# Softmax reciprocals: a 128x512 broadcast turned by four transposes, against 8 columns turned once and spread through DRAM

## The chip, the core and the metric

The kernel runs on one core of a Trainium2 chip. A core has five engines, each with a queue of its own that it works through in order: TensorE (PE, matrix products and transposes; its weight loads are shown apart as PEld), VectorE (DVE), ScalarE (ACT), GpSimd (POOL) and SyncE (SP), which here issues nearly all DMAs. Engines wait for one another and for DMAs through semaphores. The metric is the time of one execution in microseconds (us), the median over several runs.

## The reference

One layer of a hybrid encoder on 512 tokens of width 1024. Two branches run side by side: a gated linear recurrence (RG-LRU) in both directions, and 16 heads of neighbourhood attention over an 8 x 64 grid (each head has 64 channels). Both are gated, projected, merged, projected again and added to the input. The part that the change touches is the end of the attention branch:

```python
s = jnp.einsum('bqhd,bwqkhd->bhqwk', q_r, k_win).astype(jnp.float32) * scale
...
s = s + jnp.transpose(bias, (0, 2, 1, 3)).astype(jnp.float32)[None]
p = jax.nn.softmax(s.reshape(B, H, GRID_W, win_r * WIN_C), axis=-1)
...
y_b = neighbourhood_attention(qh, kh, vh, rpb[l]) * jax.nn.silu(zb)
y_b = y_b @ w_pb[l]
```

A softmax divides by the sum of its exponentials. The kernel puts this division off: it multiplies `silu(zb)` by half the reciprocal of the sum, and that by the unnormalised product of exponentials and values.

## The kernel before

Activations lie transposed in SBUF: channels on the 128 partitions, the 512 tokens along a row. Every large matrix product is made of three passes over operands split into a high and a low part, 24 instructions of 128x512 for a projection of 128 channels (tile `acc` in PSUM, weights `whi` and `wlo`, which come from `wraw`: loaded by SP, rounded by ACT, the rest subtracted by POOL or DVE).

The attention runs over eight pairs of heads; "head 0" to "head 7" below are these pairs (`pr` in the code). For each pair there are three projections (q, k and z), then the function `attention`: the scores (`sp`, 24 products), then four blocks of 16 columns of the grid. A block's scores get their bias and their row maximum on DVE (L771, tile `p`, two instructions, one for each head of the pair), exponential and sum on ACT (L777; the sums go into `sm`, 8 columns: 4 blocks x 2 heads), are transposed on PE (L786, tile `pt`, four transposes), split by ACT and DVE (`pp`, L791 and L793) and multiplied by the values (`pv`). DVE adds up the parts of the product into `yt`.

The sums lie with the block's 128 queries on the partitions, and are needed with the channels there: for the 64 channels of a head the same row of reciprocals. Before, `rc` (L825, DVE) is the reciprocal of the 8 sums; ACT copies it to `rcx`, each column repeated 64 times, 128x512 (L829); four transposes on PE turn it into `rcb` in PSUM (L834; the profile calls the tile `mi` by its class); and DVE multiplies `sz`, the gate from z, by it (L836, `szr`), then by `yt` (L838). The result is split into `ybh` and `ybl` (tile `ybhl`), which the projection with w_pb reads after all heads.

Nothing in the code fixes the order of instructions by hand. Every piece of work is an `op` with an engine, an assumed cost, a rank and the tiles that it reads and writes; a planner (class `Plan`) simulates the engines with these costs, PSUM and SBUF slots and the DMA queue, and at each step takes from each engine's ready list the first by rank of those that could begin soonest. What it settles on is the fixed program order of each engine. PE's projections have the last rank (1000 and up) and so fill what the attention leaves. A DMA is an `op` on SP; the planner assumes for it a landing by its size and what was issued before, and an `op`'s `late` adds to what its readers are planned to wait. At run time SP issues in program order; it also waits until the DMA issued eight before has landed.

Loads around the change, all on SP through `load` (L329 to L332): `wraw` (weights), `braw` (bias, read by POOL into `nb`, L712) and `vt`, the values of the next two heads, read back from DRAM where they were put as `vscr`.

Of the kernel before, what the change touches and what calls it, by code (L numbers as in the profile page):

```python
# [8 lines left out]
F32 = mybir.dt.float32  # L9
F32R = mybir.dt.float32r  # L10
AF = mybir.ActivationFunctionType
ALU = mybir.AluOpType

P = 128
# [54 lines left out]
class Plan:  # L69
# [18 lines left out]
    def op(self, eng, cost, fn, rank, r=(), w=(), rw=(), lock=False, after=(), spare=0, size=0, until=None, late=0.0, name=""):  # L88
        o = Op()
        o.alts = {eng: cost} if isinstance(eng, str) else dict(zip(eng, cost))  # L90
        o.fn, o.rank, o.lock, o.spare, o.size, o.name = fn, rank, lock, spare, size, name
        o.n, o.until, o.late = len(self.ops), until, late
        deps = set()
        for t in list(r) + list(rw):
            for f in t.family():
                deps.update(f.writers)
        for t in list(w) + list(rw):
            for f in t.family():
                deps.update(f.readers)
        for t in r:  # L100
            t.readers.append(o)
        for t in w:
            t.writers.append(o)
        for t in rw:
            for f in [t] + t.parts:
                f.writers, f.readers = [], []
            t.writers = [o]
        o.tiles = list(dict.fromkeys(t.base or t for t in list(w) + list(rw) + list(r)))
        for t in o.tiles:
            t.uses += 1  # L110
        o.data, o.succ, o.t = set(deps), [], 0.0
        deps.update(after)
        o.left = len(deps)
        for d in deps:
            d.succ.append(o)
        self.ops.append(o)
        return o
# [155 lines left out]
def act(n, ptr=0, acc=False):  # L273
    return 0.19 + 0.833e-3 * n + 0.093 * ptr + 0.19 * acc


def dve(n):
    return 0.153 + 1.043e-3 * n
# [15 lines left out]
def layer(ctx, tc, x, par, w_m, w_g, bc_gate, w_v, w_in, w_blk, rpb, amask, w_pa, w_pb, w_o, g_final, out):  # L294
    nc = tc.nc
# [4 lines left out]
    dp = ctx.enter_context(tc.tile_pool(name="dp", bufs=1, space=bass.MemoryType.DRAM))  # L300
    pl = Plan({"s": NS, "w": NW, "bank": 8}, LIMITS)
    op = pl.op
# [6 lines left out]
    def T(name, dt=F32):  # L309
        return pl.tile("s", lambda i: sb.tile([P, S], dt, tag=f"s{i}", name=nm(name)))  # L310
# [15 lines left out]

    ENGINE = {"PE": nc.tensor, "ACT": nc.scalar, "DVE": nc.vector, "POOL": nc.gpsimd, "SP": nc.sync}

    def load(t, dst, src, rank, size, after=(), spare=0, r=(), name="load"):  # L329

        return op("SP", 0.45, lambda e: nc.sync.dma_start(dst(), src() if callable(src) else src), rank,  # L331
                  r=r, w=[t], after=after, spare=spare, size=size, name=name)  # L332

    def cast(o, i):

# [17 lines left out]
    def const(name, shape, dt=F32):  # L353
# [18 lines left out]
       r=[par_sb, ident], w=[pp0])  # L372
# [78 lines left out]
    for t in range(NT):  # L451
        i = t // 2
        for h, (q, qp) in enumerate(((qa, qap), (qd, qdp))):
            j = T("junk")

            def square(e, t=t, h=h, q=q, j=j):
# [6 lines left out]
               lock=True, name="sq")  # L463
# [268 lines left out]
    def attention(pr, q, k, z, nbt, pos):  # L732
# [23 lines left out]
        def half(b0):  # L756
# [68 lines left out]
        op("DVE", 0.17, lambda e: nc.vector.reciprocal(rc.ap, sm.ap), pos - 0.3, r=[sm], w=[rc], name="rc")  # L825


        rx_ = T("rcx")
        op("ACT", act(512), lambda e: nc.scalar.activation(rx_.ap.rearrange("p (b c) -> p b c", b=8),  # L829
           rc.ap.unsqueeze(2).to_broadcast([P, 8, 64]), AF.Copy, scale=0.5), pos - 0.3, r=[rc], w=[rx_], name="rcx")  # L830

        def f(e_):
            for b in range(4):
                nc.tensor.transpose(rcb.ap[:, b * P:(b + 1) * P], rx_.ap[:, b * P:(b + 1) * P], ident.ap)  # L834
        op("PE", 0.47, f, pos - 0.3, r=[rx_, ident], w=[rcb], name="rcb")
        op("DVE", dve(512), lambda e: nc.vector.tensor_tensor(rbc(sz.ap), rbc(sz.ap), nat(rcb.ap), op=ALU.mult),  # L836
           pos - 0.3, r=[rcb], rw=[sz], name="szr")
        op("DVE", dve(512), lambda e: nc.vector.tensor_tensor(rbc(sz.ap), nat(yt.ap), rbc(sz.ap), op=ALU.mult), pos + 0.5, r=[yt],  # L838
           rw=[sz], lock=True, name="yb")
        ybh[pr], ybl[pr] = two("ybhl")  # L840
# [410 lines left out]
```

## Time and profile before

| | |
|---|---|
| median of 3 runs | 571.52 us (570.95 to 571.83) |
| the profiled execution's own time | 571.63 us |
| its span in the trace | 569.8 us |
| mean granted TensorE clock | 0.997 of full speed |
| moved by DMA | 81.35 MB, of it 6.29 MB written to DRAM |
| the eight `rc` | at 87.7 us, then every 22.4 us, the last at 243.8 us |
| PE busy, first 76 us | 73.13 us |
| PE busy, last 69.8 us | 62.56 us |

The span runs from the first to the last instruction; the rest of the execution's time lies around it. A line of the profile names a group of instructions by line of the kernel, engine, operation and tile ("out<-in", buffer numbers left out), with its count and times; what stands behind "<-" in brackets is what ended the engine's idle time before it.

### The profile page before, as it was taken

The page shows a single profiled execution, that of the slowest core. Times are in us where ns is not written, and L with a number is a line of the kernel's source. Part 1 is how long each engine was busy: PE and PEld are TensorE (multiplying, and loading weights), DVE is VectorE, ACT ScalarE, POOL GpSimd, SP SyncE. Part 2 cuts the span into 40 slices and gives each one's busy share as a digit, 9 for nine tenths or more (in the row PEclk, how much of TensorE's full clock was granted, in tenths as well). Part 3 has the DMA queues.
Part 4 walks back from the last instruction along what each step waited for, and adds up shares of the span by engine and source line. Part 5 has one row for each costly group of instructions (what it writes and reads, how often), then busy time and mean ns, then how long its engine had stood idle before and what let it go on. Part 6 is the DMA issues. An engine that isn't in the chain of part 4 may idle for free.

```text
span 569.8 us, 7748 instructions
## 1 busy us (share of the span) xinstructions
PE 559.7 (98%) x2835; PEld 463.8 (81%) x2835; DVE 392.8 (69%) x689; ACT 337.2 (59%) x585; POOL 99.5 (17%) x84
## 2 busy tenths in 40 slices
PE   8999999999999999999999999999999999999994
PEld 8787888888888888887887887787788888888884
DVE  5999966576575667886489559749847996498323
ACT  7755536747547557478938867984894433243142
POOL 0006518265374380000000000000000000000220
PEclk9999999999999999999999999999999999999998
DMA  8993978552444322132232323223238712380002
GB/s 313 409 402 115 353 220 249 163 154 106 130 121 139 93 93 75 39 126 77 74 111 93 96 76 107 74 75 110 75 114 310 276 46 103 126 316 2 0 38 112
DMA packets 30813, 81.35 MB, mean 143 GB/s; under 512 B 3263, under 2 KB 6455, under 8 KB 30775
## 3 DMA queue, kind: packets, MB, share of 16 engines
q1 hardware_dynamic: 30496, 80.53, 41.3%
q8 instruction: 22, 0.36, 0.3%
q10 hardware_dynamic: 279, 0.32, 0.2%
q14 instruction: 16, 0.13, 0.1%
HBM read 74.55 MB, written 6.29 MB: 142 GB/s over the span
## 4 chain that ended last, share of the span: by engine, by line
PE 93%; DMA 3%; DVE 2%; ACT 1%; SPq 0%; issue 0%; DVEq 0%
PE acc L342 77%; PE hx L342 6%; PE pv L342 3%; DMA wv<-in_w_v_dram 3%; PE pt L786 2%; PE gt L342 2%; PE sp L342 2%; PE mi L834 1%; DVE hhl L339 1%; SPq L331 0%; DVE wc L544 0%; DVE vl L339 0%; DVE wlo L339 0%; ACT xT L336 0%; ACT vh L336 0%
## 5 line engine op out<-in xcount | busy, mean ns | idle before, releaser
L342 PE MATMUL acc<-hhl,whi 128*128 128x512 f32 x784 | 245.9, 395 | 0.0
L342 PEld LDWEIGHTS acc<-hhl,whi 128*128 128x128 f32 x784 | 142.7, 188 | 29.0 <-issue 1.8
L342 PE MATMUL acc<-hhl,wlo 128*128 128x512 f32 x392 | 152.9, 390 | 0.0
L342 PEld LDWEIGHTS acc<-hhl,wlo 128*128 128x128 f32 x392 | 73.6, 188 | 15.9
L336 ACT CAST whi<-wraw 128x1024 fp32r<-128x1024 f32 x72 | 74.2, 1045 | 3.3 <-DMA wraw<-in_w_in_dram 2.5
L339 DVE TENSOR_TENSOR wlo<-wraw,whi 128x1024 fp32r<-128x1024 f32 x49 | 59.6, 1227 | 14.0 <-ACT whi L336 13.2
L1120 POOL TENSOR_TENSOR yo<-yo,gfin 128x512 f32<-128x512 f32 x6 | 8.2, 1359 | 338.3 <-ACT xr L1117 338.3
L339 POOL TENSOR_TENSOR wlo<-wraw,whi 128x1024 fp32r<-128x1024 f32 x23 | 55.5, 2414 | 65.7 <-ACT whi L336 37.5
L777 ACT ACTIVATE p<-p,mn 128x192 f32<-128x192 f32 (+1 forms) x64 | 30.4, 477 | 29.3 <-DVE mn L771 29.3
L712 POOL TENSOR_TENSOR nb<-msk,braw 128x192 f32<-128x192 f32 (+1 forms) x48 | 35.6, 773 | 55.6 <-DMA braw<-in_rpb_dram 55.6
L771 DVE CUSTOM_DVE_ANT_0 p<-sp,nb 128x192 f32<-128x192 f32 (+1 forms) x64 | 31.0, 611 | 17.1 <-PE sp L342 17.1
L342 PE MATMUL acc<-woh,mhl 128*128 128x512 f32 (+1 forms) x144 | 40.4, 365 | 0.0
L342 PE MATMUL acc<-yahl,whi 128*128 128x512 f32 x128 | 39.4, 389 | 0.0
L342 PE MATMUL acc<-ybhl,whi 128*128 128x512 f32 x128 | 39.4, 389 | 0.0
L997 DVE SCALAR_TENSOR_TENSOR gm<-gm,acc 128x512 f32<-128x512 f32 x16 | 11.0, 688 | 39.4 <-PE acc L342 39.4
L793 DVE TENSOR_TENSOR pp<-pt,pp 96x512 fp32r<-96x512 f32 (+1 forms) x32 | 22.0, 689 | 22.1 <-ACT pp L791 21.9
L342 PE MATMUL hx<-vh,hhl 128*128 128x512 f32 x112 | 35.5, 392 | 0.5 <-DVE hhl L339 0.5
L342 PEld LDWEIGHTS acc<-woh,mhl 128*128 128x128 f32 x144 | 26.1, 189 | 4.4
L342 PEld LDWEIGHTS acc<-yahl,whi 128*128 128x128 f32 x128 | 24.0, 188 | 5.0
L342 PEld LDWEIGHTS acc<-ybhl,whi 128*128 128x128 f32 x128 | 24.0, 188 | 5.0
L342 PE MATMUL acc<-wol,mhl 128*128 128x512 f32 (+1 forms) x72 | 26.3, 365 | 0.0
L342 PEld LDWEIGHTS hx<-vh,hhl 128*128 128x128 f32 x112 | 21.0, 188 | 5.2 <-DVE hhl L339 0.9
(195 smaller groups left out, 982.0 us busy)
## 6 DMA issues: line engine op xcount, KB each, us to landing
wraw<-in_w_in_dram SPq DMA_DIRECT2D x56, 512.0 KB
wc<-in_w_m_dram SPq DMA_DIRECT2D x16, 512.0 KB
vscr<-va SPq DMA_DIRECT2D x8, 512.0 KB
vt<-vscr SPq DMA_DIRECT2D x16, 256.0 KB
wraw<-in_w_pb_dram SPq DMA_DIRECT2D x8, 512.0 KB
wraw<-in_w_pa_dram SPq DMA_DIRECT2D x8, 512.0 KB
wr<-in_w_g_dram SPq DMA_DIRECT2D x16, 256.0 KB
wo<-in_w_o_dram SPq DMA_DIRECT2D x8, 512.0 KB
```

What stands on the lines that cost most here:

```text
L336: return lambda e: nc.scalar.copy(o(), i()) if e == "ACT" else nc.vector.tensor_copy(o(), i())
L339: return lambda e: ENGINE[e].tensor_tensor(o(), a(), b().bitcast(F32), op=ALU.subtract)
L342: nc.tensor.matmul(o, a, b, start=first, stop=last)
L712: nc.gpsimd.tensor_tensor(o, mv, view, op=ALU.subtract)
L771: nc.vector.tensor_tensor_reduce(out=o, in0=v(spv(h, e)[:, :nk]), in1=v(hv(nb)[:, h, :nk]), scale=1.0, scalar=3e38, op0=ALU.add, op1=ALU.m ...
L777: nc.scalar.activation(hv(pt_)[:, h, :nk], hv(pt_)[:, h, :nk], AF.Exp, bias=mn.ap[:, h:h + 1], scale=-1.0, accum_out=sm.ap[:, 2 * b + h:2 ...
L786: nc.tensor.transpose(pv4()[:4 * w, h, j, :], hv(pt_)[:, h, j * 4 * w:(j + 1) * 4 * w], ident.ap)
L793: op("DVE", dve(512), lambda e_, w=w, ppv=ppv, pv4=pv4: nc.vector.tensor_tensor(ppv()[:4 * w, :, :, 1, :], pv4()[:4 * w], ppv()[:4 * w, :, ...
L834: nc.tensor.transpose(rcb.ap[:, b * P:(b + 1) * P], rx_.ap[:, b * P:(b + 1) * P], ident.ap)
L997: op("DVE", dve(512), lambda e: nc.vector.scalar_tensor_tensor(t.ap, t.ap, 1.0, o.ap, op0=ALU.add, op1=ALU.mult), n - 1.9, r=[o], rw=[t], ...
L1120: op(("DVE", "POOL"), (dve(w), pool_(w)), lambda e: ENGINE[e].tensor_tensor(y(), y(), gfin[n].ap[:, gs], op=ALU.mult), rank + 0.1, r=[gfin ...
```

## The change

The broadcast copy on ACT, the four transposes and the product's PSUM operand go. In their place `rc` itself, 128 x 8, is transposed once (L830, PE, into 8 rows of the same PSUM tile `mi`); ACT copies the 8 rows to `rct` in SBUF, times 0.5 (L831); SP stores them as 4 KB to a DRAM buffer of the head, `rscr` (L833); and two loads, one for each head of the pair, read them back into `rcx` (L331), each with the head's four rows repeated over its 64 partitions, 128 KB each. The product `szr` reads `rcx` from SBUF (L837). It is marked `lock`, which has the planner keep it apart from POOL's work, and the two loads are planned as ready 1.0 us after their assumed landing (`late`). `load` passes `late` on.

```diff
-    def load(t, dst, src, rank, size, after=(), spare=0, r=(), name="load"):
+    def load(t, dst, src, rank, size, after=(), spare=0, r=(), late=0.0, name="load"):
...
-        rx_ = T("rcx")
-        op("ACT", act(512), lambda e: nc.scalar.activation(rx_.ap.rearrange("p (b c) -> p b c", b=8),
-           rc.ap.unsqueeze(2).to_broadcast([P, 8, 64]), AF.Copy, scale=0.5), pos - 0.3, r=[rc], w=[rx_], name="rcx")
-
-        def f(e_):
-            for b in range(4):
-                nc.tensor.transpose(rcb.ap[:, b * P:(b + 1) * P], rx_.ap[:, b * P:(b + 1) * P], ident.ap)
-        op("PE", 0.47, f, pos - 0.3, r=[rx_, ident], w=[rcb], name="rcb")
-        op("DVE", dve(512), lambda e: nc.vector.tensor_tensor(rbc(sz.ap), rbc(sz.ap), nat(rcb.ap), op=ALU.mult),
-           pos - 0.3, r=[rcb], rw=[sz], name="szr")
+        rct, rcx = T("rct"), T("rcx")
+        scr = pl.fixed(dp.tile([8, P], F32, name=f"rscr{pr}"))
+        op("PE", 0.15, lambda e: nc.tensor.transpose(rcb.ap[:8, :P], rc.ap, ident.ap), pos - 0.3, r=[rc, ident], w=[rcb], name="rcb")
+        op("ACT", 0.3, lambda e: nc.scalar.activation(rct.ap[:8, :P], rcb.ap[:8, :P], AF.Copy, scale=0.5), pos - 0.3, r=[rcb], w=[rct],
+           name="rct")
+        op("SP", 0.5, lambda e: nc.sync.dma_start(scr.ap, rct.ap[:8, :P]), pos - 3, r=[rct], w=[scr], size=4096, name="rcs")
+        for h in range(2):
+            src = bass.AP(scr.ap.tensor, scr.ap.offset + h * P, [[0, 64], [2 * P, 4], [1, P]])
+            load(rcx, lambda h=h: rcx.ap[H[h], :].rearrange("p (b q) -> p b q", b=4), src, pos - 3, 131072, r=[scr], name="rcl", late=1.0)
+        op("DVE", dve(512), lambda e: nc.vector.tensor_tensor(rbc(sz.ap), rbc(sz.ap), nat(rcx.ap), op=ALU.mult),
+           pos - 0.3, r=[rcx], rw=[sz], lock=True, name="szr")
```

The planner makes a new order of it. Three places follow, before and after; the numbers in the names are those of the program's tiles.

SP, the loads around head 0's reciprocals (`vt` are the values of heads 2 and 3, `wraw` the next weights). Before:

```order
L331 DMA braw_998<-in_rpb_dram 128x1x256 x2
L331 DMA vt_1009<-vscr_86 96x1x512
L331 DMA vt_1013<-vscr_86 96x1x512
L331 DMA vt_1021<-vscr_86 128x1x512
L331 DMA vt_1027<-vscr_86 128x1x512
L331 DMA vt_1034<-vscr_86 128x1x512
L331 DMA vt_1042<-vscr_86 128x1x512
L331 DMA vt_1052<-vscr_86 96x1x512
L331 DMA vt_1058<-vscr_86 96x1x512
L331 DMA wraw_1064<-in_w_in_dram 128x1024
```

After:

```order
L331 DMA braw_1010<-in_rpb_dram 128x1x256 x2
L331 DMA vt_1021<-vscr_86 96x1x512
L833 DMA rscr_88<-rct_1019 8x128
L331 DMA vt_1033<-vscr_86 96x1x512
L331 DMA vt_1040<-vscr_86 128x1x512
L331 DMA vt_1046<-vscr_86 128x1x512
L331 DMA vt_1051<-vscr_86 128x1x512
L331 DMA vt_1059<-vscr_86 128x1x512
L331 DMA rcx_1064<-rscr_88 64x4x128 x2
L331 DMA vt_1074<-vscr_86 96x1x512
L331 DMA vt_1080<-vscr_86 96x1x512
L331 DMA wraw_1086<-in_w_in_dram 128x1024
```

The store stands behind the first `vt`, five `vt` stand between it and the two loads that read it back, and two more and the weights behind those. At head 1 the store stands between the `wraw` that were issued at 99.89 us and after, at head 2 four `vt` and a `wraw` stand between store and loads.

DVE, between head 2's last block and the scores of head 3 (`yt` and `sz` are head 2's; `kl` is the low part of k, `p` and `mn` the first score block, both of head 3). Before:

```order
L836 TENSOR_TENSOR sz_1428<-sz_1428,mi_1552 128x512
L811 TENSOR_TENSOR vp_1585<-pv_1560,vp_1585 64x256
L811 TENSOR_TENSOR vp_1585<-pv_1561,vp_1585 64x256
L814 TENSOR_TENSOR yt_1545<-pv_1560,vp_1585 64x256
L814 TENSOR_TENSOR yt_1545<-pv_1561,vp_1585 64x256
L838 TENSOR_TENSOR sz_1428<-yt_1545,sz_1428 128x512
L740 SCALAR_TENSOR_TENSOR kl_1620<-acc_1510,kh_1614 128x512
L339 TENSOR_TENSOR ybhl_1623<-sz_1428,ybhl_1623 128x512
L771 ISA p_1668,mn_1669<-sp_1634,nb_1343 128x8x24
```

After:

```order
L811 TENSOR_TENSOR vp_1587<-pv_1566,vp_1587 64x256
L811 TENSOR_TENSOR vp_1587<-pv_1567,vp_1587 64x256
L814 TENSOR_TENSOR yt_1515<-pv_1566,vp_1587 64x256
L814 TENSOR_TENSOR yt_1515<-pv_1567,vp_1587 64x256
L740 SCALAR_TENSOR_TENSOR kl_1635<-acc_1517,kh_1628 128x512
L837 TENSOR_TENSOR sz_1436<-sz_1436,rcx_1605 128x512
L839 TENSOR_TENSOR sz_1436<-yt_1515,sz_1436 128x512
L771 ISA p_1679,mn_1680<-sp_1643,nb_1342 128x8x24
```

`szr` moves from ahead of the last block's sums to behind `kl`, with the second product at its heels and the next head's scores behind both. At head 0 two score instructions (the first block) stand ahead of it.

PE, the end of head 0 (`pt` is the last block, `acc` a projection of head 1). Before:

```order
L786 MATMUL pt_985<-ident,p_918 96x128 x4
L342 MATMUL acc_994<-hh_260,whi_780 128x512
L342 MATMUL acc_994<-hl_277,whi_780 128x512
L342 MATMUL acc_994<-hh_260,wlo_789 128x512
L342 MATMUL acc_994<-hhl_348,whi_780 128x512 x2
L342 MATMUL acc_994<-hhl_348,wlo_789 128x512
L342 MATMUL acc_994<-hhl_396,whi_780 128x512 x2
L342 MATMUL acc_994<-hhl_396,wlo_789 128x512
L342 MATMUL acc_994<-hhl_439,whi_780 128x512 x2
L342 MATMUL acc_994<-hhl_439,wlo_789 128x512
L834 MATMUL mi_1036<-ident,rcx_1011 128x128 x4
L342 MATMUL pv_1044<-pp_967,vt_771 128x256
```

After:

```order
L830 MATMUL mi_993<-ident,rc_988 8x128
L786 MATMUL pt_997<-ident,p_926 96x128 x4
L342 MATMUL acc_1006<-hh_268,whi_788 128x512
L342 MATMUL acc_1006<-hl_285,whi_788 128x512
L342 MATMUL acc_1006<-hh_268,wlo_797 128x512
L342 MATMUL acc_1006<-hhl_356,whi_788 128x512 x2
L342 MATMUL acc_1006<-hhl_356,wlo_797 128x512
```

The one transpose stands ahead of the last block's `pt`, where the four stood twelve products behind it. Up to head 0 and behind head 7 the orders of all engines are the same but for such shifts of a few rows.

More of the change, by code (lines that the diff above doesn't have):

```diff
@@ L327, in layer @@
     ENGINE = {"PE": nc.tensor, "ACT": nc.scalar, "DVE": nc.vector, "POOL": nc.gpsimd, "SP": nc.sync}
-    def load(t, dst, src, rank, size, after=(), spare=0, r=(), name="load"):
+    def load(t, dst, src, rank, size, after=(), spare=0, r=(), late=0.0, name="load"):
         return op("SP", 0.45, lambda e: nc.sync.dma_start(dst(), src() if callable(src) else src), rank,
-                  r=r, w=[t], after=after, spare=spare, size=size, name=name)
+                  r=r, w=[t], after=after, spare=spare, size=size, late=late, name=name)
     def cast(o, i):
```

## The prediction

> **What bounds the kernel now.** I read the page's busy shares and chain first, then the table of busy time by stretch, then what TensorE (PE) waited for.
>
> ```profile
> span 569.8 us, 7748 instructions
> PE 559.7 (98%) x2835; PEld 463.8 (81%) x2835; DVE 392.8 (69%) x689; ACT 337.2 (59%) x585; POOL 99.5 (17%) x84
> PE 93%; DMA 3%; DVE 2%; ACT 1%; SPq 0%; issue 0%; DVEq 0%
> ...
> 76.00:96.00 20.00, 20.00 (x123) 16.83 (x122) 11.68 (x32) 12.30 (x30) 9.72 (x11) 1.00 0.86 240
> 136.00:156.00 20.00, 20.00 (x122) 16.74 (x121) 12.59 (x32) 11.41 (x28) 9.44 (x10) 1.00 0.32 93
> 236.00:256.00 20.00, 20.00 (x116) 16.41 (x113) 16.02 (x37) 14.86 (x34) 0.00 (x0) 1.00 0.24 84
> ...
> PE mi L483 <- POOL onesc L360: 1.5, 1, 1.5
> PE hx L342 <- ACT xT L336: 0.9, 1, 0.9
> PE hx L342 <- DVE hhl L339: 0.5, 1, 0.5
> ```
>
> After the label, a stretch row gives its length and the busy time of PE, PEld, DVE, ACT and POOL, then granted clock, DMA share and GB/s. In the stretches where the edited code runs (heads 0 to 7, about 77 to 256 us) PE is busy 20.00 of 20.00 us at full clock, and the three waits listed for PE are 2.9 us in the whole run and belong to the start (hx and the warm-up). DVE and ACT have a fifth to two fifths of their time free there. So in this region the kernel lasts as long as PE's stream of instructions: PE work taken out shortens the time by its length, and work on other engines counts only if it makes PE wait. Behind this region the instruction order is not changed, and PE stays busy until its last product, so what is saved is carried to the end.
>
> **The change, part by part.**
>
> *Removed from PE, added to PE.* The page's chain, in order of time, shows what a transpose costs in this stream (start, length):
>
> ```profile
> 85.96 0.44 PE pt L786 x4
> ...
> 88.96 0.44 PE pt L786 x4
> 89.39 2.75 PE acc L342 x12
> 92.15 0.44 PE mi L834 x4
> ...
> L834 PE MATMUL mi<-ident,rcx x32: 270/272/273, 92.0 to 248.4; 128*128 128x128 f32 x32
> ```
>
> The group of four at 92.15 is the one that goes, eight times: 8 x 0.44 = 3.52 us. (The 272 ns of one are a pipelined duration; four take 0.44 us, 0.11 each.) One 8-column transpose per head comes in. No row shows one alone; its weight load has 8 columns, its moving operand is the same 128x128 identity. The bounds are 0 (it slips in beside its neighbours) and 0.272 us (nothing overlaps). The nearest row is the group itself, 0.11 each, and I take that: 8 x 0.11 = 0.88 us. Net: 3.52 - 0.88 = **2.64 us less PE stream**; the bounds give 3.52 and 3.52 - 2.18 = 1.34.
>
> The loads of 96 and of 128 weight columns do differ, but the groups do not get shorter:
>
> ```profile
> L786 PEld LDWEIGHTS pt<-ident,p 128*128 128x128 f32 x64 | 7.7, 141 | 1.1
> L786 PEld LDWEIGHTS pt<-ident,p 128*96 128x96 f32 x64 | 7.5, 125 | 2.2
> ```
>
> The group at 85.96 has 128 weight columns, that at 88.96 has 96; both take 0.44 us. So the weight load is not what spaces transposes, and 8 columns should not buy much. The Trainium skill (TensorE: Matmul & The Clock Gate, "Step-by-step: what each phase is for") says that loading weights takes time by the number of columns. The 125 against 141 ns agree in direction, the equal groups say that it does not reach the stream; if it did, the lone transposes would fall towards the lower bound and the gain would be up to 3.52 us.
>
> *ACT and DVE.* The 128x512 copy gives way to an 8x128 one, which has its like at the start:
>
> ```profile
> L829 ACT ACTIVATE rcx<-rc x8: 630/632/635, 90.0 to 246.9; 128x512 f32<-128x512 f32 x8
> 0.74 0.66 ACTq L361 DMA_DIRECT2D par_sb<-in_par_dram  x1
> 3.87 0.31 ACT L365 ACTIVATE tan<-par_sb 8x128 f32<-8x128 f32 x1 [0.95 <-DMA par_sb<-in_par_dram]
> L836 DVE TENSOR_TENSOR sz<-sz,mi 128x512 f32<-128x512 f32 x8 | 5.4, 677 | 0.6 <-PE mi L834 0.6
> L838 DVE TENSOR_TENSOR sz<-yt,sz 128x512 f32<-128x512 f32 x8 | 5.6, 700 | 0.3
> ```
>
> ACT saves 0.32 us per head; the first product with sz now reads SBUF on both sides, like the second one: 23 ns more per head. Both lie beside PE's projections and are costed at nothing; were that cover gone, they would be 0.2 us of loss against 2.6 of gain.
>
> *The added wait: two DMA trips in a row.* The reciprocals go to DRAM (store `rscr`), and only when that has landed are they read back (`rcx`, two loads). Nobody but the product `szr` (L837) needs them, but DVE works in order: behind a waiting `szr` stand the score blocks of the next head, and behind those the exponentials, the `pt` transposes and PE. A trip in an empty queue is the par_sb pair above: issued at 0.74, used at 3.87, 3.1 us. In the busy stretch it is longer:
>
> ```profile
> 77.26 1.28 SPq L331 DMA_DIRECT2D braw<-in_rpb_dram  x2
> 79.07 1.30 SPq L331 DMA_DIRECT2D wraw<-in_w_in_dram  x3
> 80.42 2.85 SPq L331 DMA_DIRECT2D braw<-in_rpb_dram  x2
> 83.31 11.03 SPq L331 DMA_DIRECT2D vt<-vscr  x8
> 94.39 1.57 SPq L331 DMA_DIRECT2D wraw<-in_w_in_dram  x3
> ...
> 99.89 3.78 SPq L331 DMA_DIRECT2D wraw<-in_w_in_dram  x3
> 114.46 1.28 SPq L331 DMA_DIRECT2D braw<-in_rpb_dram  x2
> ...
> 85.82 2.79 POOL L712 TENSOR_TENSOR nb<-msk,braw 128x256 f32<-128x256 f32 x5 [3.46 <-DMA braw<-in_rpb_dram]
> ...
> 90.00 0.63 ACT L829 ACTIVATE rcx<-rc 128x512 f32<-128x512 f32 x1
> 100.74 0.52 DVE L771 CUSTOM_DVE_ANT_0 p<-sp,nb 128x192 f32<-128x192 f32 x1 [2.29 <-PE sp L342]
> 101.11 0.54 DVE L771 CUSTOM_DVE_ANT_0 p<-sp,nb 128x192 f32<-128x192 f32 x1
> ...
> 104.63 0.50 ACT L777 ACTIVATE p<-p,mn 128x256 f32<-128x256 f32 x1
> 106.59 0.60 PE L786 MATMUL pt<-ident,p 128*128 128x128 f32 x4
> ```
>
> The second `braw` of 77.26 is issued at about 77.9 and released POOL at 85.82: 7.9 us. Two trips plus 0.7 us for the second load's issue are thus an estimated 3.1 + 0.7 + 3.1 = 6.9 us in an empty queue and 7.9 + 0.7 + 7.9 = 16.5 us in a full one. I take both ends to the three tightest places.
>
> Head 0: `rct` stands where ACT had `rcx` at 90.00, so the store can go at 90.3. `szr` stands behind two score blocks, that is at about 101.5: 11.2 us later. This is between the ends and nearer the empty one, and a reason stands beside it: SP itself waits from the first `vt` (issued by 84.1) to 90.3, so for 6 us nothing is put into the queue, and it can drain to the level of those first transfers before the store. I forecast that `szr` does not wait, or for less than PE's own margin: the exponential of the second block ended at 104.63 + 0.50 = 105.13, its `pt` began at 106.59, 1.46 us later.
>
> Head 2: `szr` stands straight behind `kl` and ahead of all score blocks. Its store goes after the lone transpose, which by the PE rows falls some 14 us after that head's scores (122.08 in the trace), so near 136.3; then SP issues four `vt` and a `wraw` before the loads, and they land near 143.4 (empty) or 148.2 (trips with those five ahead of them at 7.9). `szr` and the product behind it take 1.4 us, so the score blocks, at 145.53 before, begin on time or 4 us late; the new PE order has 24 `acc` instead of 15 ahead of that head's first `pt` (9 x 0.23 = 2.05 us) on top of a margin like the one above. No wait in the first case, about half a microsecond in the second.
>
> The DMA share falls from 0.86 to 0.32 by the stretch from 136 us on, and the other heads have score blocks or output products ahead of `szr`, so the near end holds there. Taken: **0 us**.
>
> *SP's queue.* The store waits on SP for `rct`, and the loads behind it wait with it. Worst are the last two `wraw` of 99.89, held from about 100.4 until head 1's `rct`, some 15 us. They are loads 13 and 14 of w_in and are cast in the order of loading:
>
> ```profile
> 135.84 1.05 ACT L336 CAST whi<-wraw 128x1024 fp32r<-128x1024 f32 x1
> 139.59 1.05 ACT L336 CAST whi<-wraw 128x1024 fp32r<-128x1024 f32 x1
> ```
>
> Issued by 119 and 7.9 us under way they are there by 127, 9 us ahead. The `vt` behind head 0's store serve heads 2 and 3, 30 us on. The DMAs add 16 x 128 KB = 2 MB to 81. Taken: 0 us; if this cover failed, a projection's first `acc` would wait for its weights.
>
> **Sum.** The profiled execution took 571.63 us (span 569.8 and 1.83 around it), 0.11 over the median of 571.52. 571.63 - 2.64 + 0 = 568.99: **569.0 us**, 0.46% less.
>
> **Rivals.**
>
> (a) *Lone transposes nearly free.* PE's gain goes to 3.52 us: 568.1. For: the load has a sixteenth of the columns. Against: the two equal groups. Chance 0.1. The Trainium skill's rule on columns, cited above, speaks for it.
>
> (b) *The transposes filled time that PE has to spend anyway*, waiting for softmax: the order now has other `acc` in their place, but if the chain sp, scores, exponential, `pt` sets the pace, or late `szr` eats the gain piece by piece, nothing is left: 571.6, or up to 1 us less. For: the margins of 1.5 us per step are small. Against: PE busy 20.00 of 20.00 and no wait listed after the start. Chance 0.14.
>
> (c) *The round trip makes DVE wait and PE with it; slower.* Place: head 0, in the stretch with DMA at 0.86. With both trips at 7.9 us the loads land 16.5 us after 90.3, at 106.8, 5.3 us after `szr`'s turn; less the 1.46 of margin, PE stands 3.8 us, and with half a microsecond at head 2 it is 569.0 + 4.3 = 573.3. It decides once PE stands over 2.64 us in all, that is, if head 0's loads land after about 105.6. The Trainium skill (DMA: Bandwidth & Descriptors, "Anatomy of one DMA — SWDGE (gpsimd) path") puts most of a transfer's fixed cost of some 2 us, for transfers issued by GpSimd, in the confirmation that the data landed, DRAM being slowest; a read-back pays it twice. The 3.1 us above agree with such a floor; by two floors alone `szr` would be in time. Chance 0.1.
>
> **How the numbers follow.** Forecast 0.66 at 568.6 to 570.3 (a microsecond of small waits included), (a) 0.10, (b) 0.14, (c) 0.10. A range from 568.1 (a) to 571.6 (b) leaves out little but (c). 0.2% of this kernel, 1.1 us, is about what a measurement can tell from no change: faster is the forecast and (a), 0.76; within it (b), 0.14; slower (c), 0.10.
>
> **What would show it.** Right: the PE group on `mi` falls from 32 to 8 instructions, each standing in the chain with 0.1 us, PE is still busy 20.00 of 20.00 up to 256 us, and the scores of the last head begin about 2 us earlier. DVE's idle time ahead of `sz` on `rcx` is below 2 us in all. Wrong: waits of PE on `p` or `pp`, idle time of DVE named to DMA `rcx` of more than 3 us at head 0 or 2, `whi` waiting for `wraw` after 100 us, or a chain that no longer is PE alone in this region.

## The result and the profile after

| | before | after |
|---|---|---|
| median | 571.41 us (570.82 to 571.83, 6 runs) | 568.50 us (567.48 to 569.44, 6 runs) |
| ratio | | 0.9950, 95% interval 0.9938 to 0.9961 |
| profiled execution | 571.63 us | 567.48 us |

The change makes the kernel 2.91 us faster; 569.0 was forecast. The medians agree to half a microsecond, but the sum behind the forecast does not hold term by term: one term came out as forecast, and two others, which nearly cancel, were not in it.

The page of the changed kernel, span, busy time and the chain that ended last:

```profile
span 565.5 us, 7733 instructions
PE 557.2 (99%) x2811; PEld 461.2 (82%) x2811; DVE 388.5 (69%) x689; ACT 333.6 (59%) x585; POOL 94.2 (17%) x84
...
PE 95%; DMA 3%; SPq 0%; ACT 0%; DVE 0%; issue 0%
```

PE has 24 instructions fewer, and the chain is still PE. What PE waited for, and what DVE waited for at the new product (us in total, times, longest):

```profile
PE mi L483 <- POOL onesc L360: 1.5, 1, 1.5
PE hx L342 <- ACT xT L336: 0.4, 1, 0.4
```
```profile
DVE sz L837 <- DMA rcx<-rscr: 4.9, 1, 4.9
```

PE waits only at the start. DVE waits once for the read-back, 4.9 us, at head 2, and PE loses nothing by it in this execution. The transposes, by their tile and in the chain in order of time:

```profile
L830 PEld LDWEIGHTS mi<-ident,rc x8: 83/84/87, 87.8 to 246.8; 128*8 128x8 f32 x8
L830 PE MATMUL mi<-ident,rc x8: 271/272/273, 88.0 to 247.0; 128*8 128x128 f32 x8
```
```profile
87.45 0.69 PE acc L342 x3
88.14 0.11 PE mi L830
88.25 0.44 PE pt L786 x4
```

The weight load of 8 columns takes 84 ns where 128 columns took 141, but the transpose takes 0.11 us of PE's stream, as one of a group of four does.

How long did the edited region get? The timeline of PE has three marks: the first score product of head 0 (`sp`), the first product behind the heads (`gt`), and the last product of the program. Before, then after:

```profile
77.21 0.36 PE L342 MATMUL sp<-kh,qh 64*128 64x192 f32 x2
...
252.98 0.50 PE L342 MATMUL gt<-xh,gwh 64*128 64x512 f32 x2
...
562.28 0.28 PE L342 MATMUL acc<-woh,mhl 128*128 128x256 f32 x1
```
```profile
76.43 0.36 PE L342 MATMUL sp<-kh,qh 64*128 64x192 f32 x2
...
249.56 0.50 PE L342 MATMUL gt<-xh,gwh 64*128 64x512 f32 x2
...
558.88 0.28 PE L342 MATMUL acc<-woh,mhl 128*128 128x256 f32 x1
```

The heads take 252.98 - 77.21 = 175.77 us before and 249.56 - 76.43 = 173.13 after: 2.64 us less, which is the forecast's net term to the hundredth. From `gt` to the last product it is 309.30 and 309.32: what was saved is carried to the end, as the prediction said. The spans differ by 4.3 us and not by 2.64, because two stretches outside the heads differ too: the start (77.21 against 76.43, which moves between 76.4 and 77.7 from one profile to the next, whatever the kernel), and the end, from the last product to the end of the span: 569.8 - 562.28 = 7.5 us before, 565.5 - 558.88 = 6.6 after. The stretch of the heads is therefore the measure for the experiments below.

### The profile page after: what moved, and what is told of

Same layout as the page of the kernel before. It is cut to its first block, busy times and chain, and to the rows that moved or that the text cites. A ratio compares the mean times of both kernels' runs of the same rounds, so it can differ in the third digit from the quotient of the medians.

```text
span 565.5 us, 7733 instructions
## 1 busy us (share of the span) xinstructions
PE 557.2 (99%) x2811; PEld 461.2 (82%) x2811; DVE 388.5 (69%) x689; ACT 333.6 (59%) x585; POOL 94.2 (17%) x84
## 4 chain that ended last, share of the span: by engine, by line
PE 95%; DMA 3%; SPq 0%; ACT 0%; DVE 0%; issue 0%
PE acc L342 78%; PE hx L342 7%; PE pv L342 3%; DMA wv<-in_w_v_dram 3%; PE pt L786 2%; PE gt L342 2%; PE sp L342 2%; SPq L331 0%; ACT vh L336 0%; PE mi L342 0%; PE mi L830 0%; PE hx L443 0%; DVE yo L1142 0%; ACT xT L336 0%; DVE yo L1110 0%
## 5 line engine op out<-in xcount | busy, mean ns | idle before, releaser
L712 POOL TENSOR_TENSOR nb<-msk,braw 128x192 f32<-128x192 f32 (+1 forms) x48 | 30.3, 664 | 54.3 <-DMA braw<-in_rpb_dram 54.3
L342 PE MATMUL acc<-yahl,wlo 128*128 128x512 f32 x64 | 24.9, 389 | 0.0
```

What stands on the lines that cost most here:

```text
L342: nc.tensor.matmul(o, a, b, start=first, stop=last)
L712: nc.gpsimd.tensor_tensor(o, mv, view, op=ALU.subtract)
```

## The experiments

In all expectations, Theory A is the prediction's: PE's stream sets the time and the trip through DRAM is hidden. "Stretch" is the time from the first `sp` to the first `gt` in the profiled execution.

### The transposes by themselves

Four 8-column transposes a head in the changed kernel, its order otherwise kept:

```diff
-        op("PE", 0.15, lambda e: nc.tensor.transpose(rcb.ap[:8, :P], rc.ap, ident.ap), pos - 0.3, ...)
+        def f(e_):
+            for b in (3, 2, 1, 0):
+                nc.tensor.transpose(rcb.ap[:8, b * P:(b + 1) * P], rc.ap, ident.ap)
+        op("PE", 0.15, f, pos - 0.3, ...)
```

> The changed kernel with the transpose of the 8 columns made four times per head (three more into unused parts of the same PSUM tile), the order of all other instructions unchanged. Theory A (the gain is PE stream, 0.109 us per transpose): 24 transposes come back, +2.6 us against the changed kernel, about 571.1 us, ratio to the kernel before 0.9995 (0.998 to 1.001). Theory B (the gain came from the new order or from the shorter work of ACT): no change against the changed kernel, 568.5 us, ratio 0.995.

Measured: 570.95 us against 571.05, ratio 0.9993 (0.9984 to 1.0001); stretch 175.77 us, exactly that of the kernel before. Four narrow transposes cost PE what four wide ones cost.

One 128-column transpose a head in the kernel before, with its broadcast copy, its order and no trip through DRAM:

```diff
         def f(e_):
-            for b in range(4):
-                nc.tensor.transpose(rcb.ap[:, b * P:(b + 1) * P], rx_.ap[:, b * P:(b + 1) * P], ident.ap)
+            nc.tensor.transpose(rcb.ap[:, :P], rx_.ap[:, :P], ident.ap)
...
```

DVE's product (not shown) reads the first block's reciprocals for all four blocks; the kernel leaves out those of the other three.

> The kernel before, in its own order and without DRAM, with one transpose of 128x128 per head in place of four; the reciprocals of the first block serve all four blocks (the other three are left out). Theory A: 24 transposes of 0.109 us go, -2.6 us, about 568.8 us, ratio 0.9954 (0.994 to 0.997), the same as the whole change. Theory B (the new order made the gain, or transposes filled time that PE must spend anyway): 571.4 us, ratio 1.000.

Measured: 568.64 us (568.53 to 569.09), ratio 0.9956 (0.9943 to 0.9969); stretch 173.47 us, 2.30 less than before. So most of the gain, 2.30 of 2.64 us, comes with the number of transposes, and needs neither the narrow operand nor the new order. The lone transpose stands in this kernel's chain with 0.11 us as well, so that 24 fewer should save 2.6; where the other 0.3 us went was not traced. Rival (a), lone transposes nearly free, falls with these two runs; rival (b), transposes that filled time PE had to spend anyway, falls too.

### How close the trip through DRAM is to hurting

First, with no lateness planned for the two loads, so that the planner puts `szr` ahead of all score blocks of the next head at seven heads (by the changed kernel's trace it stands so at three, heads 2, 5 and 6, and not at one, as the expectation has it):

```diff
-            load(rcx, ..., name="rcl", late=1.0)
+            load(rcx, ..., name="rcl", late=0.0)
```

> The changed kernel with the 1.0 us of planned lateness of the two loads set to 0: the planner puts the product with sz ahead of all score blocks of the next head in seven of eight heads (one before). Theory A with margins: DVE waits for the loads longer (up to 2 us per head), PE does not, 568.5 us, ratio 0.995 (0.993 to 0.997). Theory C: every wait of DVE reaches PE, about 1 us per head, 573 to 577 us.

Measured: 568.10 us (567.26 to 568.20), ratio 0.9940 (0.9928 to 0.9952). DVE now waits 9.8 us for `rcx`, at three heads, 3.6 at most, and PE's stretch is 173.03 us. The waits are longer than the 2 us expected, and nearly 10 us of idle DVE still cost nothing.

Then a slower trip: `rc`, halved by a small DVE instruction, is stored as it lies, without any transpose or copy on ACT, in 1,024 pieces of 4 bytes.

```diff
-        op("SP", 0.5, lambda e: nc.sync.dma_start(scr.ap, rct.ap[:8, :P]), pos - 3, r=[rct], ...)
+        op("SP", 0.5, lambda e: nc.sync.dma_start(scr.ap.rearrange("k q -> q k"), rc.ap), pos - 3, r=[rc], ...)
```

> No transpose at all: the halved reciprocals, 128x8, are stored straight to DRAM as 8 rows in 1024 pieces of 4 bytes, and read back as in the changed kernel; one small DVE instruction more per head. Theory A with the round trip hidden: 8 transposes fewer, -0.9 us against the changed kernel, about 567.6 us, ratio to before 0.9934 (0.992 to 0.995). Theory C (the trip is at the edge of its cover): the store of small pieces takes some us longer, DVE waits at the product with sz and PE with it; each us beyond a margin of 1.5 us costs a us per head, 570 us or more.

Measured: 654.16 us, ratio 1.146 (1.1433 to 1.1486). Theory A missed, by 87 us; its rival's "570 us or more" held. By the store's tile, PE's waits and the page's row of the granted clock:

```profile
L831 SPq DMA_DIRECT2D rscr<-rc x8: 377/377/378, 88.6 to 321.9; - x8
...
DMA to landing us min/median/max: 9.9/11.1/11.7
```
```profile
PE sp L342 <- DVE kl L740: 64.0, 7, 11.5
```
```profile
PEclk9999996988889798979899999999999999999999
```

The store lands after 11.1 us. For the 8 rows of 512 bytes of the changed kernel, SP's timeline gives the bound: store issued at 157.50 at head 3, the loads that wait for it at 158.77.

```profile
157.50 0.29 SPq L833 DMA_DIRECT2D rscr<-rct  x1
158.77 1.29 SPq L331 DMA_DIRECT2D rcx<-rscr  x2
```

That is 1.27 us, for the same 4 KB. The Trainium skill (DMA: Bandwidth & Descriptors, "Why small descriptors are slow (HBM only)") gives each descriptor a fixed overhead; the direction agrees, and the size here is 11.1 against 1.27 us. The one transpose that the change keeps is worth its 0.11 us: it turns 4-byte pieces into rows.

The 87 us are not the price of the trip alone. Without the transpose the planner makes another order, and in it `szr` stands ahead of `kl` at every head that has a next one; in the changed kernel it does so at head 6 only. So a late `szr` holds up the next head's scores themselves, the 64.0 us of waits above. DVE, at head 1 of this kernel:

```profile
143.03 2.42 DVE L835 TENSOR_TENSOR sz<-sz,rcx 128x512 f32<-128x512 f32 x1 [10.70 <-DMA rcx<-rscr]
...
145.94 0.69 DVE L740 SCALAR_TENSOR_TENSOR kl<-acc,kh 128x512 fp32r<-128x512 f32 x1
```

To find the edge, the next four kernels keep the changed kernel's program order (SP's copies apart) and move only the landing of `rcx`. One lets the loads leave without the store:

```diff
-            src = bass.AP(scr.ap.tensor, scr.ap.offset + h * P, [[0, 64], [2 * P, 4], [1, P]])
+            src = bass.AP(x.tensor, x.offset + h * P, [[0, 64], [2 * P, 4], [1, P]])
```

> The changed kernel in the same program order, but the two loads of rcx read a constant buffer (the input x) in place of rscr, so they no longer wait until the store has landed; the store itself stays (the values multiplied into sz are then not the reciprocals). Theory A (the time follows PE's stream, the trip through DRAM is hidden): as the changed kernel, 568.5 us, ratio 0.994 to 0.996, PE's stretch from head 0's first score to the first product behind the heads 173.1 us; DVE's idle time on rcx falls from 4.9 us to under 2, and nothing comes of it. Rival C (part of the gain is lost to the trip's wait): faster than the changed kernel, by up to the 4.9 us of DVE's wait, 564 to 567.5 us, ratio under 0.993.

The others put one, three and six copies from DRAM to DRAM behind the store (shown for one):

```diff
+        hop = [dp.tile([8, P], F32, name=f"hop{pr}_{i}") for i in range(1)]
+        def f(e_):
+            nc.sync.dma_start(hop[0], rct.ap[:8, :P])
+            for i in range(1, 1):
+                nc.sync.dma_start(hop[i], hop[i - 1])
+            nc.sync.dma_start(scr.ap, hop[-1])
```

> The changed kernel in the same program order, with one copy DRAM to DRAM of the 4 KB put between the store and the read-back, which the planner does not know of: SP waits for it and the loads leave later by one more landing, an estimated 1.2 to 3 us (the store's own landings in the changed kernel's trace). The product szr began 0.1 to 3.4 us after its loads had landed, so DVE would wait up to 2 us at six of the eight heads and longer at head 2. Theory A (hidden, PE has more margin than the 1.5 us of the prediction): 568 to 569.5 us, ratio 0.993 to 0.997, DVE idle on rcx 10 to 20 us in all, PE waits under 1 us. Rival C (each microsecond of late szr beyond about 1.5 us is one of PE): 569.5 to 572 us.

> As the kernel with one hop, with three copies DRAM to DRAM in a row: the loads leave an estimated 4 to 9 us later, SP stands as long, DVE waits for rcx at every head, 3 to 6 us each, 25 to 50 us in all. Theory A with a margin of about 4 us a head (the longest wait seen so far without a wait of PE is 4.9 us at head 2): 569 to 575 us, PE waits on p or sp 0 to 6 us in all. Rival C with a margin of 1.5 us: 2 to 4 us lost at each head, 584 to 600 us, ratio 1.02 to 1.05. If the prediction's decision point for its slower rival is right (head 0's loads landing after about 105.6 us), PE's first wait at head 0 comes only when the loads land later than that.

> As before, with six copies in a row: the loads leave an estimated 8 to 18 us later than in the changed kernel. By both theories PE must now stand. Theory A with a margin of 4 us a head: 4 to 10 us lost at most heads, 590 to 640 us, ratio 1.03 to 1.12; DVE idle on rcx 60 to 120 us. If DVE's idle time is that long and the time stays under 575 us, the score blocks do not set PE's pace at all and both are wrong.

| kernel | median, us | ratio and interval | stretch, us | DVE idle on rcx |
|---|---|---|---|---|
| no wait for the landing | 569.01 | 0.9957 (0.9945 to 0.9969) | 174.52 | 6.2 |
| one hop | 569.66 | 0.9973 (0.9963 to 0.9984) | 175.06 | 7.5 |
| three hops | 596.13 | 1.0451 (1.0418 to 1.0484) | 199.68 | 38.0 |
| six hops | 645.25 | 1.1293 (1.1276 to 1.1309) | 241.86 | 79.3 |

With one hop the time lies at the low end of its rival's range, and DVE's idle time below the 10 to 20 us of theory A. With three hops the time and the idle time are within the rival's ranges (a margin of 1.5 us), above theory A's. With six the idle time is as expected, and the time is above theory A's 590 to 640 us.

The first kernel was to have less waiting, and had more: the expectation on DVE's idle time missed. At head 2 its loads did not leave earlier (four `vt` and a `wraw` stand ahead of them on SP in any case) and they landed later; they also read another buffer, `x`, and whether that delayed them was not tried. Its stretch is 1.39 us longer than the changed kernel's 173.13, although its trip has one dependence less. What DVE and PE did there, by the timelines of that kernel (in brackets the idle time before and what ended it):

```profile
147.03 0.69 DVE L837 TENSOR_TENSOR sz<-sz,rcx 128x512 f32<-128x512 f32 x1 [6.19 <-DMA rcx<-in_x_dram]
```
```profile
151.03 0.87 PE L786 MATMUL pt<-ident,p 128*96 128x128 f32 x4 [0.90 <-ACT p L777]
```

`szr` began 1.3 us later than in the changed kernel, counted from head 0's first `sp`, and PE stood. (The loss is more than the 0.90 us of idle time: the last `acc` ahead counts as busy for 0.39 us, where the next would follow after 0.23, and the four `pt` spread over 0.87 us instead of 0.60.) And this is how the changed kernel got through, by the timelines of DVE, ACT and PE:

```profile
145.53 0.69 DVE L837 TENSOR_TENSOR sz<-sz,rcx 128x512 f32<-128x512 f32 x1 [4.87 <-DMA rcx<-rscr]
146.25 0.69 DVE L839 TENSOR_TENSOR sz<-yt,sz 128x512 f32<-128x512 f32 x1
146.86 0.53 DVE L771 CUSTOM_DVE_ANT_0 p<-sp,nb 128x192 f32<-128x192 f32 x1
```
```profile
146.98 0.62 ACT L336 CAST ybhl<-sz 128x512 fp32r<-128x512 f32 x1 [7.04 <-DVE sz L839]
147.51 1.04 ACT L336 CAST whi<-wraw 128x1024 fp32r<-128x1024 f32 x1
148.46 0.59 ACT L822 ACTIVATE sz<-acc 128x512 f32<-128x512 f32 x1
148.94 0.45 ACT L777 ACTIVATE p<-p,mn 128x192 f32<-128x192 f32 x1
...
149.38 0.44 ACT L777 ACTIVATE p<-p,mn 128x192 f32<-128x192 f32 x1
```
```profile
149.80 0.60 PE L786 MATMUL pt<-ident,p 128*96 128x128 f32 x4
```

The second exponential ends at 149.82, and `pt` starts at 149.80: there is no margin left at all. The late product holds up two engines. Behind it on DVE stand the score blocks, as the prediction said. On ACT stands the cast of its result, `ybhl<-sz`, idle 7.04 us for it, and behind that a weight cast, a tanh of `sz`, and only then the exponentials: 148.94 - 146.86 = 2.1 us from the first score block on DVE to the first exponential. In the kernel before it is 146.14 - 145.53 = 0.6 us:

```profile
145.53 0.52 DVE L771 CUSTOM_DVE_ANT_0 p<-sp,nb 128x192 f32<-128x192 f32 x1 [2.29 <-PE sp L342]
...
146.14 0.46 ACT L777 ACTIVATE p<-p,mn 128x192 f32<-128x192 f32 x1 [3.76 <-DVE mn L771]
146.60 0.44 ACT L777 ACTIVATE p<-p,mn 128x192 f32<-128x192 f32 x1
...
149.54 0.60 PE L786 MATMUL pt<-ident,p 128*96 128x128 f32 x4
```

There the second exponential ended at 147.04, and `pt` had 2.5 us to spare.

Across the profiles of one program order, loss and lateness go together. The start of head 2's `szr` is counted from head 0's first `sp` of the same execution:

| kernel | profiled execution, us | szr of head 2, us | stretch, us |
|---|---|---|---|
| loads straight behind the store (below) | 567.53 | 64.15 | 173.16 |
| changed kernel | 567.48 | 69.10 | 173.13 |
| changed kernel again (below) | 568.21 | 69.81 | 173.89 |
| no wait for the landing | 569.05 | 70.42 | 174.52 |
| one hop | 570.49 | 70.97 | 175.06 |

From 69.81 on, 1.16 us of lateness are 1.17 us of stretch, and the line meets 173.13 at 69.05. The profiled execution of the changed kernel stood within a tenth of a microsecond of its edge; it was the fastest of its six. In the second profile of the same kernel PE stands 0.3 us for `p` at head 2.

With three hops DVE waits at every head, and PE six times. PE's waits, the windows around its first stand at head 0 (length, busy PE, PEld, DVE, ACT and POOL, granted clock, DMA share, GB/s), and its timeline there:

```profile
PE pv L342 <- DVE pp L793: 9.6, 4, 4.6
PE pt L786 <- ACT p L777: 4.9, 1, 4.9
PE sp L342 <- DVE kl L740: 2.0, 1, 2.0
```
```profile
100.00:106.00 6.00, 6.00 (x46) 5.08 (x45) 0.90 (x4) 0.99 (x4) 0.35 (x1) 1.00 0.95 235
...
112.50:117.20 4.70, 4.42 (x14) 3.75 (x15) 2.19 (x8) 2.68 (x8) 3.01 (x2) 0.50 0.57 189
```
```profile
112.78 1.22 PE L342 MATMUL pv<-pp,vt 96*128 96x256 f32 x4 [4.55 <-DVE pp L793]
...
115.51 0.63 PE L342 MATMUL acc<-hhl,wlo 128*128 128x512 f32 x1
115.94 1.05 PE L342 MATMUL acc<-hhl,whi 128*128 128x512 f32 x2
```

PE's waits are 16.5 us in all, and the stretch grew by 199.68 - 173.13 = 26.6. The other 10 us are clock: PE was busy for 183.14 us of this stretch, at a mean granted clock of 0.95, with the instructions that took 173.13 in the changed kernel. After the stand of 4.55 us the granted clock is 0.50 over the next 4.7 us, and products come 0.43 us apart (115.51 to 115.94) where they came 0.23 apart. The Trainium skill (TensorE: Matmul & The Clock Gate, "What's actually happening") has this: half rate after some 3.4 us of idle time, full rate after as long a busy one. The run agrees, and the stands of 0.9 and 1.4 us in the two shorter kernels are not followed by such a fall (mean clock 0.996 and 0.998 over these executions).

### The edge taken away

If head 2's landing is what spreads the changed kernel's executions from 567.5 to 569.4 us, its loads have to leave earlier. The last variant issues at every head the two loads straight behind their store, and what SP had between them after; all other engines keep the changed kernel's order.

```diff
+    held = []
+
     def load(t, dst, src, rank, size, after=(), spare=0, r=(), late=0.0, name="load"):
-        return op("SP", 0.45, lambda e: nc.sync.dma_start(dst(), src() if callable(src) else src), rank,
+        def go(e):
+            start = lambda: nc.sync.dma_start(dst(), src() if callable(src) else src)
+            if held and name != "rcl":
+                held.append(start)
+                return
+            start()
+            if name == "rcl":
+                held[0] += 1
+                if held[0] == 2:
+                    rest = held[1:]
+                    held.clear()
+                    for g in rest:
+                        g()
+        return op("SP", 0.45, go, rank,
...
-        op("SP", 0.5, lambda e: nc.sync.dma_start(scr.ap, rct.ap[:8, :P]), pos - 3, ...)
+        op("SP", 0.5, lambda e: (nc.sync.dma_start(scr.ap, rct.ap[:8, :P]), held.append(0)), pos - 3, ...)
```

> The changed kernel with one thing moved: on SP the two loads of rcx go straight behind their store at every head (the five vt at head 0, the four vt and the wraw at head 2, and one wraw each at heads 1 and 4, that stood between, are issued behind them); the order of all other engines is that of the changed kernel. Theory E (head 2 is at its edge: in the profiled run of the changed kernel szr began at 145.53 us without PE standing, in the run without the landing wait 1.3 us later and PE stood 1.3; so part of the changed kernel's executions lose up to about 1.5 us there): the loads of head 2 land about 4 us earlier, near 141, DVE's wait on rcx falls below 1.5 us, and the median comes to 567.2 to 567.9 us, 0.5 to 1 us below the changed kernel on the same chip, with executions that lie closer together. Rival N (the spread of the changed kernel, 567.5 to 569.4, comes from elsewhere): the median stays at that of the changed kernel, within 0.3 us.

> The changed kernel once more, on the same chip as its variants: 567.5 to 569.5 us, median near 568.5, ratio 0.994 to 0.996. Theory E: in the profiled run PE's stretch from head 0's first score to the first product behind the heads is 173.1 us plus whatever szr at head 2 came later than 69.1 us after head 0's first score; rival N: no such relation.

> The kernel with no planned lateness once more, on the same chip: its loads at head 2 left 1.1 us earlier than the changed kernel's and szr began 1.8 us earlier against head 0's first score, so that by theory E it is off the edge in most executions: 567.3 to 568.2 us, some 0.4 us below the changed kernel; by rival N the same as the changed kernel within 0.3 us.

| kernel, on one chip | median, us | lowest to highest, 5 runs | ratio and interval |
|---|---|---|---|
| loads straight behind the store | 567.63 | 567.53 to 567.94 | 0.9934 (0.9922 to 0.9947) |
| changed kernel again | 568.89 | 568.03 to 569.51 | 0.9954 (0.9942 to 0.9967) |
| no planned lateness again | 567.99 | 567.28 to 568.70 | 0.9940 (0.9926 to 0.9954) |

The intervals of the first two overlap a little; the executions themselves do not: the slowest of the first is below the fastest of the second. SP's queue at head 2 by the timeline, in the variant and in the changed kernel:

```profile
134.79 0.30 SPq L848 DMA_DIRECT2D rscr<-rct  x1
136.13 1.26 SPq L334 DMA_DIRECT2D rcx<-rscr  x2
137.44 2.97 SPq L334 DMA_DIRECT2D vt<-vscr  x4
```
```profile
134.53 0.30 SPq L833 DMA_DIRECT2D rscr<-rct  x1
134.94 3.71 SPq L331 DMA_DIRECT2D vt<-vscr  x4
138.70 0.50 SPq L331 DMA_DIRECT2D wraw<-in_w_in_dram  x1
139.30 1.30 SPq L331 DMA_DIRECT2D rcx<-rscr  x2
```

The loads leave 3.2 us earlier, no idle time of DVE on `rcx` is left, and `szr` begins at 140.83. (It takes 2.09 us there instead of 0.69, with POOL at work from 139.99 to 142.37; it still ends some 3 us earlier. No run tests what stretches it.) Theory E's rule gives 173.8 us for the stretch of the changed kernel's second profile, and 173.89 was measured.

How much a typical execution of the changed kernel loses at head 2 is less sure. The profiled executions of the two kernels differ by 0.73 us of stretch (173.89 against 173.16), the medians by 1.26 us. About 0.2 us of the 1.26 lie outside the spans, and the start, which moves by more than a microsecond between profiles, is not known for the other executions. The variant moves loads at heads 0, 1 and 4 as well, but within the heads the second profile shows no wait of PE except that at head 2. So a typical execution loses 0.7 to 1.3 us there, on this chip; the fastest ones lose nothing. The kernel without planned lateness shows 0.9 us less than the changed kernel, but its executions overlap with both others: for it, the test is weak.

### The end of the program

The stretch from the last product to the end was 6.6 us in every kernel with the trip and its usual store, 7.3 to 7.5 in the two without a trip. The last kernel adds the 24 DMAs to the kernel before:

```diff
+        def g(e_):
+            nc.sync.dma_start(scr.ap, rx_.ap[:8, :P])
+            for h in range(2):
+                src = bass.AP(scr.ap.tensor, scr.ap.offset + h * P, [[0, 64], [2 * P, 4], [1, P]])
+                nc.sync.dma_start(dump.ap[H[h], :].rearrange("p (b q) -> p b q", b=4), src)
+        op("SP", 0.5, g, pos - 3, r=[rx_], w=[scr, dump], size=4096, name="rcs")
```

> The kernel before, with its four transposes and the order of all its engines, plus the changed kernel's 24 DMAs on SP: at each head the store of 4 KB (8 rows of rcx) behind the copy L829 and the two read-backs of 128 KB straight behind it, into a tile that nobody reads. Two theories on the end: in all kernels with these DMAs the stretch from the last product to the end took 6.5 to 6.6 us, in the two without them 7.2 to 7.5, though the same work stands there. Theory T (the end follows SP's program, of which the 24 DMAs are a part): the stretch becomes 6.5 to 6.6 us and the median 570.3 to 570.8 us, ratio 0.998 to 0.9992. Theory U (it follows something else in the changed kernels): 7.2 to 7.5 us and 571.2 to 571.6 us, ratio 0.9995 to 1.0005. By both, the trip itself costs PE nothing: its stretch from head 0's first score to the first product behind the heads stays 175.8 us.

Measured: 570.45 us against 571.18, ratio 0.9990 (0.9981 to 0.9999). Its span and the marks of PE's timeline:

```profile
span 568.3 us, 7781 instructions
```
```profile
76.65 0.36 PE L342 MATMUL sp<-kh,qh 64*128 64x192 f32 x2
...
252.41 0.50 PE L342 MATMUL gt<-xh,gwh 64*128 64x512 f32 x2
...
561.71 0.28 PE L342 MATMUL acc<-woh,mhl 128*128 128x256 f32 x1
```

The stretch is 175.76 us as before: 24 DMAs, 2 MB, in these stretches cost PE nothing. The end takes 568.3 - 561.71 = 6.6 us. So DMAs that nobody uses make the kernel 0.7 us faster (the interval reaches from 0.1 to 1.1), through its end: 0.9 us less in the span, of which 0.3 come back outside it (2.15 us around the span, 1.86 before). Of the 0.9 us, 0.5 lie in SP's wait for the last of the output's transfers (2.6 us before, 2.1 here and in the changed kernel). How 24 earlier instructions on SP shorten the end was not tried.

## Why the prediction was right, and where not

**PE's stream, -2.64 us: right.** 175.77 to 173.13, and 0.11 us for a lone transpose, both as forecast. The step from the two equal `pt` groups to "8 columns should not buy much" is what the run with four narrow transposes shows, and the run with one wide transpose shows most of the rest, 2.30 us: the count sets the gain, but for 0.3 us that stay open. ACT's and DVE's edits at nothing: right, since the run with the old copy has the gain as well.

**Head 0: right, with less room than thought.** `szr` began at 100.3 without a wait. The prediction's quiet trip of 6.9 us was too long (in the variant above the loads follow the store by 1.3 to 2.2 us where 3.1 were assumed, and a load takes 3.3 at the median), but five `vt` stand between store and loads, which left at 93.95. With one hop they left 0.85 us later, counted from head 0's first `sp`, and DVE waited 0.18 us here.

The rival's price came out in its number: with three hops the loads landed at 108.0 by the trace; its working puts `szr`'s turn at 101.5, or 102.0 on this execution's clock (head 0 began 0.5 us later), and less 1.46 of margin PE should stand 4.5 us. It stood 4.55. Its path did not: PE stood on `pv` for `pp`, the split of a block whose scores are ahead of `szr`, and not on `pt` for the next block's exponential. So the agreement is luck. What the rival also lacked is the half clock behind such a stand, another 2 us.

**Head 2: the step that failed.** The prediction had the loads land between 143.4 and 148.2; DVE began `szr` at 145.53, inside. (The DMA share from 136 to 156 us was 0.63 in the changed kernel, and not the 0.32 that the prediction read before: the order moves transfers too.) It granted PE 3.5 us, 2.05 for "24 `acc` instead of 15" and a margin like head 0's 1.46, and let only late score blocks draw on them. Counted from head 0's first `sp`, the first `pt` of head 3 stands at 72.33 before and at 73.37 after, 1.04 us later and not 2.05, since the transposes saved at three heads bring PE there 1.0 us earlier. But the margin before was 2.5 us at this head, not 1.46. The cover was thus 3.54 us, as granted, by two errors that cancel.

The score blocks began 2.11 us later (68.32 before, 70.43 after), which would have left 1.4 us of room. None was left: from the first score block to the end of the second exponential 2.96 us went by, where it had been 1.51. The step that failed is naming only DVE's queue behind the waiting product. ACT's was there too, with the cast of the same product ahead of the exponentials; it took these 1.45 us, which the prediction put at nothing. "No wait" is true of the fastest executions; a typical one loses 0.7 to 1.3 us. At head 5 `szr` also stands straight behind `kl`, where the prediction has score blocks or output products ahead of it; there nothing stands between store and loads on SP (200.08 and 201.36), and DVE did not wait.

**The end of the program: not in the sum.** -0.7 us (570.45 against 571.18), by the added DMAs alone.

Put together: -2.64 - 0.73 + 0.7 to 1.3 = -2.7 to -2.1 us, where -2.49 was measured beside these runs (interval -3.3 to -1.9) and -2.91 at first (-3.5 to -2.2). What remains, up to 0.8 us, is less than the width of the intervals, and no run shows a cause for it. That the forecast hit 0.5 us from the median is in part luck: the two missing terms have opposite signs.

**The signs it named.** 8 transposes of 0.11 us in the chain and PE full: seen. DVE idle on `rcx` below 2 us: wrong, 4.9 us at head 2, which the prediction called a sign against itself (over 3 us); it was a sign of the edge, not yet of a loss. A wait of PE on `p`, another sign against the prediction, is missing in the first profile and there in the second, 0.3 us at head 2. The last head's scores came 1.73 us earlier (234.69 to 232.96), of which 0.78 belongs to the earlier start: a poor mark, as the new order also moves scores among projections.

## What to carry to other kernels

On a saturated engine, count instructions and their spacing, not their duration or operand width: here four transposes cost the same whether 8 or 128 columns are loaded. When an instruction is made to wait for a DMA, list what stands behind it on its own engine and also what stands behind its *readers* on theirs; the shortest of these margins is the kernel's. A read-back is better issued straight behind its store (here five `vt` at one head, four and a `wraw` at another, stood between), and where a profiled execution is the fastest of its group, look at how far it stood from its nearest edge before believing that it has none.

## What was not expected of the hardware

The same 4 KB took at most 1.27 us to DRAM as 8 rows of 512 bytes, and 11.1 us as 1,024 pieces of 4. A stand of PE of 4.55 us halved its granted clock for the 4.7 us that followed, and with three hops the lower clock added 10 us to 16.5 us of stands. And 24 additional DMAs made the end of the program 0.9 us shorter in the profile.
